# Rotary score products over all 128 rows, and SwiGLU blocks turned by VectorE and ScalarE instead of TensorE

## The chip, the cores and the metric

The kernel runs on one core of a Trainium2 chip. The metric is the device time of one execution in microseconds (us); the times shown are medians of several runs, and one further execution was taken with the hardware profiler. Five engines appear: TensorE (PE in the profile, its weight loads PEld), VectorE (DVE), ScalarE (ACT), GpSimd (POOL) and SyncE (SP), which issues the weight loads from memory. Each engine works through its own list of instructions in the order of that list, and waits where an instruction needs another engine's result or a free buffer.

## What is computed

One layer of an encoder on 256 tokens of width 2048, all in fp32. The layer has two SwiGLU half steps with an inner width of 5632, and between them a mixer (a gated linear recurrence, and an attention with rotary positions) and a cross attention. The two parts that matter here:

```python
def swiglu_half_step(x, pre_g, w_gate, w_up, w_down, post_g):
    h = rms_norm(x, pre_g)
    y = (jax.nn.silu(h @ w_gate) * (h @ w_up)) @ w_down
    return x + FFN_RESIDUAL_WEIGHT * rms_norm(y, post_g)

...
    q_nope, q_pe = q[..., :QK_NOPE], q[..., QK_NOPE:]          # 128 and 64 columns per head, 16 heads
    q_pe = rotary(q_pe, cos[:, :, None, :], sin[:, :, None, :])
    k_pe = rotary(k_pe, cos, sin)                              # one k_pe for all heads
...
        s = jnp.einsum('bqhd,bkhd->bhqk', q_blk, k, preferred_element_type=jnp.float32) * scale
```

A head's score is thus the sum of a product over 128 features and of one over 64 rotary features.

## The kernel before

**Weights.** Every weight tile is 128 x 1024 fp32 (512 KB). `feed` loads it through SP's queue (`raw`, four buffers), ScalarE rounds it to `whi` (L98), VectorE computes the rest `wlo` = raw - whi (L99). `whi` and `wlo` have three buffers each. A product is three matmuls, high by high (L128), low by high (L129) and high by low (L130). One weight tile feeds 12 matmuls of 512 columns in `gemm`; such a dozen is called a group here. Since there are three buffers, ScalarE can round the tile of a group when TensorE has ended the group three before it.

**SwiGLU.** `ffn` goes through 22 blocks of 256 inner columns in two segments, 12 and then 10. A block is one `gemm` named `gu` of 8 groups, with gate columns in the left half of a bank and up columns in the right. ScalarE applies silu (`sg`, L285), VectorE multiplies (`h`, L286), once for each half of the tokens. The next product contracts over the inner columns, so `h` (tokens in rows) has to be turned to `hT` (inner columns in rows). Before the change TensorE does that with four 128 x 128 transposes into a PSUM bank (L290), and `part_split` makes the rounded `fh` (ScalarE, L169) and the rest `fl` (VectorE, L170). After a segment's blocks, four `gemm` named `dn` contract over all its inner columns, 12 groups each in the first segment and 10 in the second; the last block of a segment is needed in the last group of each. There are two half steps, so 44 blocks.

**Rotary scores.** `query_pe` leaves the turned rotary queries of two heads in one 128-row tile, one head in rows 0 to 63 and the other in rows 64 to 127. `key_pe` leaves the turned rotary key twice, in the upper and in the lower 64 rows of `kpeT`. `attend` handles four heads at a time. For each head and each half of the queries (128 or 256 keys) it adds two fp32 products in the same bank: one over 128 rows (L543) and one over the head's 64 rows (L544). A softmax follows on VectorE and ScalarE (L546 to L557), then TensorE transposes the probabilities (L565).

**What sets the order.** A scheduler orders each engine's list when the program is built; `high_priority` lets the weight chain go first, and `issue_after(x)` puts instructions behind instruction x in an engine's list.

Of the kernel before, what the change touches and what calls it, by code (L numbers as in the profile page):

```python
# [9 lines left out]
F32 = mybir.dt.float32  # L10
# [4 lines left out]
AF = mybir.ActivationFunctionType  # L15
# [3 lines left out]
P = 128  # L19
# [18 lines left out]
class Layer:  # L38
    def __init__(self, ctx, tc, A):
        self.tc, self.nc, self.A = tc, tc.nc, A  # L40
        nc = self.nc
        ep = lambda name, bufs, **k: ctx.enter_context(tc.tile_pool(name=name, bufs=bufs, **k))
        self.cst = ep("cst", 1)
        self.small = ep("small", 4)
        self.wraw = ep("wraw", 4)
        self.wsp = ep("wsp", 3)
        self.xp = ep("xp", 4)
        self.hp = ep("hp", 4)
        self.sl = ep("sl", 1)
        self.t2 = ep("t2", 6)  # L50
        self.jk = ep("jk", 1)
        self.gb = ep("gb", 2)
        self.pg = ep("pg", 4, space=bass.MemoryType.PSUM)
        self.pm = ep("pm", 4, space=bass.MemoryType.PSUM)
        self.n = 0
        self.plan, self.at, self.ready = [], 0, 0
        self.spare = {}
        self.last_mm = None
        self.q = []
        self.pending = []  # L60
        self.ident = self.cst.tile([P, P], F32, name="ident")
        make_identity(nc, self.ident)
        self.gc = self.cst.tile([P, NGC], F32, name="gc")
        nc.gpsimd.dma_start(out=self.gc, in_=A["gcol"])
# [20 lines left out]
    def feed(self, ahead):  # L85
        nc = self.nc
        while self.ready < min(self.at + ahead, len(self.plan)):
            src = self.plan[self.ready]
            spare = self.ready in self.spare
            n = src.shape[-1]  # L90
            raw = self.wraw.tile([P, n], F32, name=self.nm("raw"), tag="raw")
            nc.sync.dma_start(out=raw, in_=src)
            if spare:
                hi, lo = self.slot(self.spare[self.ready], "whi", F32R), self.slot(self.spare[self.ready], "wlo", F32R)
            else:
                hi = self.wsp.tile([P, n], F32R, name=self.nm("whi"), tag="whi")
                lo = self.wsp.tile([P, n], F32R, name=self.nm("wlo"), tag="wlo")
            nc.scalar.activation(hi, raw, AF.Copy)  # L98
            nc.vector.tensor_tensor(lo, raw, hi.bitcast(F32), ALU.subtract)  # L99
            self.q.append((hi, lo))  # L100
            self.ready += 1
# [9 lines left out]
    def gemm(self, act, k0, k1, name="g", head=0, tail=0, warm=0):  # L111
        nc = self.nc
        ps = [self.pg.tile([P, 512], F32, name=self.nm(name), tag="g") for _ in range(2)]
        if warm:
            self.keep_warm(ps[1], warm)
        n = (k1 - k0) // 2
        groups = ([range(head)] if head else []) + [range(i, i + 1) for i in range(head, n - tail)] + ([range(n - tail, n)] if tail else [])
        for grp in groups:
            if grp[0] >= head and (grp[0] - head) % 2 == 0:
                self.settle(1)  # L120
            w = [self.weights(self.pending and grp[0] > head) for _ in grp]
            ks = [k0 + 2 * t + c for t in grp for c in range(2)]
            order = [(k, m) for k in ks for m in range(2)] if len(ks) == 2 else [(k, m) for m in range(2) for k in ks]
            for k, m in order:
                wh, wl = w[(k - ks[0]) // 2]
                c = slice(512 * ((k - k0) % 2), 512 * ((k - k0) % 2) + 512)
                ah, al = act(k, m)
                nc.tensor.matmul(ps[m], lhsT=ah, rhs=wh[:, c], start=(k == k0), stop=False)  # L128
                nc.tensor.matmul(ps[m], lhsT=ah, rhs=wl[:, c], start=False, stop=False)  # L129
                self.last_mm = nc.tensor.matmul(ps[m], lhsT=al, rhs=wh[:, c], start=False, stop=(k == k1 - 1))  # L130
        self.settle()
        return ps
# [40 lines left out]
    def gain_split(self, hi, lo, pieces):  # L173
        nc = self.nc
        for o, ps, g in pieces:
            ins = nc.scalar.activation(hi[:, o], ps, AF.Identity, scale=self.gc[:, g : g + 1])
        for o, ps, g in pieces:
            self.last_lo = nc.vector.scalar_tensor_tensor(lo[:, o], ps, self.gc[:, g : g + 1], hi[:, o].bitcast(F32), ALU.mult, ALU.subtract)  # L178
        return ins

    def block_T(self, hi, lo, x, gcols=None, scale=None):
        for half in range(2):
# [83 lines left out]
    def ffn(self, st, which, aside=None):  # L266
        nc = self.nc
        act, r = self.halves(st[0], st[1]), st[2]
        ys = [None] * 4
        ss, ry = self.sm(8, "ssy"), []  # L270
        for si, (b0, b1) in enumerate(SEG):
            quads = []
            for b in range(b0, b1):
                ps = self.gemm(act, 0, KC, "gu", head=SKEW if b == 0 else 0, warm=WARM if b == 0 else 0)
                if (b - b0) % 2 == 0:
                    tag = "A" if len(quads) < 4 else "B"
                    hi, lo = self.slot(tag, "fh", F32R), self.slot(tag, "fl", F32R)
                    quads.append((hi, lo))
                if b == 0 and aside:
                    with self.tc.issue_after(self.last_lo.ins):  # L280
                        aside()
                h = self.tmp("h")
                for m in range(2):
                    sg = self.tmp("sg")
                    nc.scalar.activation(sg[:, :256], ps[m][:, :256], AF.Silu, scale=r[m])  # L285
                    nc.vector.scalar_tensor_tensor(h[:, m * 256 : m * 256 + 256], ps[m][:, 256:], r[m], sg[:, :256], ALU.mult, ALU.mult)  # L286
                pt = self.bank("pT")
                for c in range(2):
                    for m in range(2):
                        nc.tensor.transpose(pt[:, c * 256 + m * P : c * 256 + m * P + P], h[:, m * 256 + c * P : m * 256 + c * P + P], self.ident)  # L290
                s = slice(512 * ((b - b0) % 2), 512 * ((b - b0) % 2) + 512)
                self.part_split(hi[:, s], lo[:, s], pt)
            fa = self.halves([q[0] for q in quads], [q[1] for q in quads])
            for j in range(4):
                ps = self.gemm(fa, 0, 2 * (b1 - b0), "dn", tail=TAIL if si == 1 and j == 3 else 0)
                if si == 0:
                    ys[j] = self.slot("G", "y")
                    for m in range(2):
                        nc.scalar.activation(ys[j][:, m * 512 : m * 512 + 512], ps[m], AF.Copy)
                else:  # L300
                    g = self.load_gain(which, j)
                    for m in range(2):
                        yv = ys[j][:, m * 512 : m * 512 + 512]
                        nc.vector.tensor_tensor(yv, ps[m], yv, ALU.add)
                        ry.append(self.postnorm_block(j, m, g, yv, yv, ss, 0.5))
        return ys, ry[-2:]
# [60 lines left out]
    def mixer_consts(self):  # L367
        nc, v, c = self.nc, self.nc.vector, self.cst
# [20 lines left out]
        m, e0, e1 = (c.tile([P, 16], F32, name=n) for n in ("lbm", "lbe0", "lbe1"))  # L389
# [16 lines left out]
        v.tensor_copy(pf, pi)  # L406
        fr = c.tile([P, 32], F32, name="freq")
        nc.gpsimd.dma_start(out=fr, in_=self.A["invf"].to_broadcast([P, 32]))
        ang, n, tail, w = (c.tile([P, 64], F32, name=s) for s in ("ang", "angn", "angt", "angw"))
        for m_ in range(2):  # L410
            v.tensor_scalar(ang[:, 32 * m_ : 32 * m_ + 32], fr, pf[:, m_ : m_ + 1], None, ALU.mult)
        magic = 12582912.0
# [66 lines left out]
    def key_pe(self, act, r):  # L479
# [21 lines left out]
        pt = self.bank("pT")  # L501
        for m in range(2):
            nc.tensor.transpose(pt[:, m * P : m * P + P], k2[:, m * P : m * P + P], self.ident)
        self.kpeT = self.cst.tile([P, 256], F32, name="kpeT")
        nc.vector.tensor_copy(self.kpeT, pt[:, :256])

    def query_pe(self, ps):
        nc = self.nc
# [22 lines left out]
    def attend(self, g, qn, kn, qpe, value):  # L531
# [2 lines left out]
        probs = []  # L534
        for h in range(4):
            c = 256 * h
            rows = slice(64 * (h % 2), 64 * (h % 2) + 64)
            pc = 256 * ((4 * g + h) // 2 % 4)
            ps = self.bank("sc")
            for m, n0 in ((0, 0), (1, P)):  # L540
                w = P + P * m
                o = ps[:, n0 : n0 + w]
                nc.tensor.matmul(o, lhsT=qn[:, c + m * P : c + m * P + P], rhs=kn[:, c : c + w], start=True, stop=False)  # L543
                nc.tensor.matmul(o, lhsT=qpe[rows, pc + m * P : pc + m * P + P], rhs=self.kpeT[rows, :w], start=False, stop=True)  # L544
            s = self.tmp("s")
            nc.vector.scalar_tensor_tensor(s[:, :384], ps[:, :384], scale, self.amask, ALU.mult, ALU.add)  # L546
            mx, sums = self.sm(2, "mx"), self.sm(2, "su")
# [451 lines left out]
```

## Time and profile before

| | |
|---|---|
| median of 3 runs | 2651.07 us (2650.95 to 2651.12) |
| profiled execution | 2651.14 us, of which the span from first to last instruction is 2649.1 us |
| mean granted clock of TensorE | 0.999 of full speed |
| busy: PE / DVE / ACT / POOL | 2622.8 / 1497.3 / 1311.8 / 13.2 us |
| chain that ended last | PE 96%, DVE 2%, DMA 1%, ACT 1% |
| DMA | 481.39 MB, 182 GB/s on the mean |

The page's busy times are sums over an engine's instructions, where overlapping ones count once. A matmul's duration in a row holds the time from its start to its modelled end, and matmuls overlap; what one costs is read from the distance between starts. A row of the timeline gives the start, the length, engine, line and operation, and in brackets how long the engine was idle before, and what ended that.

### The profile page before, as it was taken

How to read it: one execution, taken by the hardware profiler on the slowest of the kernel's cores; microseconds unless marked ns; L12 is line 12 of the kernel's file. 1: busy time of each engine (PE TensorE's matmuls, PEld its weight loads, DVE VectorE, ACT ScalarE, POOL GpSimd, SP SyncE). 2: the span in 40 equal slices, each digit the busy share in tenths (PEclk: the TensorE clock that was granted, in tenths of full speed). 3: DMA queues.
4: the chain of work that ended last, by engine and by line, in shares of the span. 5: the costliest groups of instructions: out<-in, count | busy, mean ns of one | idle time of the engine just before them, and what ended most of it. 6: DMA issues, size and time to landing. Idle time of an engine off the chain costs nothing.

```text
span 2649.1 us, 33984 instructions
## 1 busy us (share of the span) xinstructions
PE 2622.8 (99%) x13136; PEld 2215.3 (84%) x13136; DVE 1497.3 (57%) x2004; ACT 1311.8 (50%) x1750; POOL 13.2 (0%) x36
## 2 busy tenths in 40 slices
PE   9999999999999999999999999999999999999998
PEld 7888888888888888889989988889788888888886
DVE  6555444554576544447577575657655554455555
ACT  5444444444455444346666664555644444444443
POOL 0000000000000000000000000000000000000000
PEclk9999999999999999999999999999999999999999
DMA  6655555555654346555545545665455556655564
GB/s 230 191 188 187 190 196 192 188 188 189 202 171 144 111 155 195 191 191 160 167 154 165 168 161 189 205 205 178 149 193 191 188 188 193 195 191 188 189 194 161
DMA packets 133714, 481.39 MB, mean 182 GB/s; under 512 B 15024, under 2 KB 15040, under 8 KB 133552
## 3 DMA queue, kind: packets, MB, share of 16 engines
q1 hardware_dynamic: 131472, 473.49, 55.4%
q0 software_dynamic: 1504, 4.68, 0.6%
q8 instruction: 103, 1.69, 0.3%
q10 hardware_dynamic: 576, 1.05, 0.1%
q14 instruction: 59, 0.48, 0.1%
HBM read 477.06 MB, written 2.10 MB: 181 GB/s over the span
## 4 chain that ended last, share of the span: by engine, by line
PE 96%; DVE 2%; DMA 1%; ACT 1%; issue 0%; SPq 0%; DVEq 0%; ACTq 0%
PE gu L130 12%; PE gu L129 12%; PE gu L128 12%; PE dn L128 6%; PE dn L129 6%; PE dn L130 6%; PE gate L130 2%; PE gate L128 2%; PE gate L129 2%; PE wo L129 1%; PE wo L130 1%; PE wo L128 1%; PE hf L352 1%; PE hf L351 1%; PE hf L350 1%; PE hv L129 1%
## 5 line engine op out<-in xcount | busy, mean ns | idle before, releaser
L99 DVE TENSOR_TENSOR wlo<-raw,whi 128x1024 fp32r<-128x1024 f32 x893 | 1092.5, 1225 | 1045.4 <-ACT whi L98 1044.3
L98 ACT ACTIVATE whi<-raw 128x1024 fp32r<-128x1024 f32 x893 | 945.9, 1060 | 1084.0 <-PE gu L130 444.9
L129 PE MATMUL gu<-wlo,hh 128*128 128x512 f32 x1408 | 552.1, 392 | 1.4 <-DVE wlo L99 1.4
L130 PE MATMUL gu<-whi,hl 128*128 128x512 f32 x1408 | 549.1, 390 | 0.7 <-DVE hl L178 0.7
L128 PE MATMUL gu<-whi,hh 128*128 128x512 f32 x1408 | 496.6, 393 | 1.8 <-ACT whi L98 1.5
L128 PEld LDWEIGHTS gu<-whi,hh 128*128 128x128 f32 x1408 | 263.9, 188 | 60.2 <-ACT whi L98 2.1
L130 PEld LDWEIGHTS gu<-whi,hl 128*128 128x128 f32 x1408 | 264.4, 188 | 55.7 <-DVE hl L178 1.5
L129 PEld LDWEIGHTS gu<-wlo,hh 128*128 128x128 f32 x1408 | 264.5, 188 | 55.0 <-DVE wlo L99 2.2
L129 PE MATMUL dn<-wlo,fh 128*128 128x512 f32 x704 | 274.2, 390 | 0.0
L130 PE MATMUL dn<-whi,fl 128*128 128x512 f32 x704 | 274.0, 389 | 0.0
L128 PE MATMUL dn<-whi,fh 128*128 128x512 f32 x704 | 247.1, 390 | 0.0
L128 PEld LDWEIGHTS dn<-whi,fh 128*128 128x128 f32 x704 | 132.1, 188 | 27.8
L130 PEld LDWEIGHTS dn<-whi,fl 128*128 128x128 f32 x704 | 132.2, 188 | 27.3
L129 PEld LDWEIGHTS dn<-wlo,fh 128*128 128x128 f32 x704 | 132.2, 188 | 27.1
L129 PE MATMUL gate<-wlo,hh 128*128 128x512 f32 x256 | 100.7, 394 | 0.0
L130 PE MATMUL gate<-whi,hl 128*128 128x512 f32 x256 | 100.1, 391 | 0.0
L128 PE MATMUL gate<-whi,hh 128*128 128x512 f32 x256 | 91.8, 391 | 0.0
L351 PE MATMUL hf<-hl,whi 128*128 128x256 f32 x256 | 72.5, 284 | 0.0
L351 PE MATMUL hq<-hl,whi 128*128 128x256 f32 x256 | 72.4, 284 | 0.0
L350 PE MATMUL hf<-hh,whi 128*128 128x256 f32 x256 | 72.3, 283 | 0.0
L350 PE MATMUL hq<-hh,whi 128*128 128x256 f32 x256 | 72.1, 283 | 0.0
L352 PE MATMUL hf<-hh,wlo 128*128 128x256 f32 x256 | 71.8, 283 | 0.0
(358 smaller groups left out, 3544.3 us busy)
## 6 DMA issues: line engine op xcount, KB each, us to landing
raw<-in_ffn_gu_dram SPq DMA_DIRECT2D x352, 512.0 KB, 3.4
raw<-in_win_dram SPq DMA_DIRECT2D x208, 512.0 KB, 3.5
raw<-in_ffn_dn_dram SPq DMA_DIRECT2D x176, 512.0 KB, 3.5
raw<-in_wbb_dram SPq DMA_DIRECT2D x32, 512.0 KB, 3.4
raw<-in_wba_dram SPq DMA_DIRECT2D x32, 512.0 KB, 3.5
raw<-in_wo_dram SPq DMA_DIRECT2D x32, 512.0 KB, 3.6
gb<-in_grow_dram POOLq DMA_DIRECT2D x16, 256.0 KB, 4.6
raw<-in_qup_n_dram SPq DMA_DIRECT2D x8, 512.0 KB, 3.4
```

Source lines behind the costliest of these rows:

```text
L98: nc.scalar.activation(hi, raw, AF.Copy)
L99: nc.vector.tensor_tensor(lo, raw, hi.bitcast(F32), ALU.subtract)
L128: nc.tensor.matmul(ps[m], lhsT=ah, rhs=wh[:, c], start=(k == k0), stop=False)
L129: nc.tensor.matmul(ps[m], lhsT=ah, rhs=wl[:, c], start=False, stop=False)
L130: self.last_mm = nc.tensor.matmul(ps[m], lhsT=al, rhs=wh[:, c], start=False, stop=(k == k1 - 1))
L350: nc.tensor.matmul(o, lhsT=wh[:, c], rhs=ah, start=first, stop=False)
L351: nc.tensor.matmul(o, lhsT=wh[:, c], rhs=al, start=False, stop=False)
L352: nc.tensor.matmul(o, lhsT=wl[:, c], rhs=ah, start=False, stop=last)
```

## The change

Two parts.

1. **SwiGLU blocks.** The four TensorE transposes of a block and their PSUM bank go. `turn` does one VectorE transpose of the 128 x 512 tile `h` to `hb`, which turns each 32 x 32 square in place, and 16 ScalarE copies of 32 rows x 128 elements, which put the squares where they belong in `hT`. The copies wait in the list `later`: four of them are issued behind the rounding of group 3's weights of the next `gemm`, four each behind those of groups 4, 5 and 6, and `part_split`, now from SBUF, behind that of group 7.
2. **Rotary scores.** `kpeT` becomes 128 x 512: left half with the key in rows 0 to 63 and zeros below, right half with zeros above and the key in rows 64 to 127. The second product runs over all 128 rows of both heads' queries, and the zeros take the other head out.

To make room, the four small tiles of the angle computation become slices of one temporary tile.

```diff
-            nc.scalar.activation(hi, raw, AF.Copy)
+            self.last_hi = nc.scalar.activation(hi, raw, AF.Copy)
...
             w = [self.weights(self.pending and grp[0] > head) for _ in grp]
+            if self.later and grp[0] >= 3:
+                with self.tc.issue_after(self.last_hi.ins):
+                    self.later.pop(0)()
...
+    def turn(self, h, hi, lo):
+        nc = self.nc
+        b, o = self.tmp("hb"), self.tmp("hT")
+        nc.vector.transpose(b, h)
+        bv = b.rearrange("p (m c q t) -> p m c q t", m=2, c=2, q=4)
+        ov = o.rearrange("p (c m x t) -> p m c x t", c=2, m=2, x=4)
+
+        def strips(x):
+            for q in range(4):
+                nc.scalar.activation(ov[32 * q : 32 * q + 32, :, :, x, :], bv[32 * x : 32 * x + 32, :, :, q, :], AF.Copy)
+
+        self.later += [lambda x=x: strips(x) for x in range(4)] + [lambda: self.part_split(hi, lo, o)]
...
-                pt = self.bank("pT")
-                for c in range(2):
-                    for m in range(2):
-                        nc.tensor.transpose(pt[:, c * 256 + m * P : c * 256 + m * P + P], h[:, m * 256 + c * P : m * 256 + c * P + P], self.ident)
                 s = slice(512 * ((b - b0) % 2), 512 * ((b - b0) % 2) + 512)
-                self.part_split(hi[:, s], lo[:, s], pt)
+                self.turn(h, hi[:, s], lo[:, s])
...
-        ang, n, tail, w = (c.tile([P, 64], F32, name=s) for s in ("ang", "angn", "angt", "angw"))
+        wk = self.tmp("ang")
+        ang, n, tail, w = (wk[:, 64 * i : 64 * i + 64] for i in range(4))
...
-        self.kpeT = self.cst.tile([P, 256], F32, name="kpeT")
-        nc.vector.tensor_copy(self.kpeT, pt[:, :256])
+
+        self.kpeT = self.cst.tile([P, 512], F32, name="kpeT")
+        nc.gpsimd.memset(self.kpeT, 0.0)
+        for h in range(2):
+            nc.vector.tensor_copy(self.kpeT[64 * h : 64 * h + 64, 256 * h : 256 * h + 256], pt[64 * h : 64 * h + 64, :256])
...
-            rows = slice(64 * (h % 2), 64 * (h % 2) + 64)
+            kc = 256 * (h % 2)
...
-                nc.tensor.matmul(o, lhsT=qpe[rows, pc + m * P : pc + m * P + P], rhs=self.kpeT[rows, :w], start=False, stop=True)
+                nc.tensor.matmul(o, lhsT=qpe[:, pc + m * P : pc + m * P + P], rhs=self.kpeT[:, kc : kc + w], start=False, stop=True)
```

TensorE's list is, instruction by instruction, the old one without the 176 transposes L290. SP's list is the same. VectorE's and ScalarE's lists change at the blocks alone, and VectorE's at `kpeT`, where two copies of 64 rows stand for one of 128. POOL gets one memset, ahead of the first gain load that has to wait.

ScalarE, from the silu of a SwiGLU block to that of the next (`whi` roundings of weights, `sg` silu, `fh` rounded inner activations), before:

```order
L285 ACTIVATE sg_807<-gu_658,ry_379 128x256
L98 ACTIVATE whi_860<-raw_858 128x1024
L285 ACTIVATE sg_810<-gu_659,ry_393 128x256
L98 ACTIVATE whi_878<-raw_876 128x1024
L98 ACTIVATE whi_896<-raw_894 128x1024
L169 ACTIVATE fh_804<-pT_813 128x512
L98 ACTIVATE whi_914<-raw_912 128x1024
L98 ACTIVATE whi_932<-raw_930 128x1024
```

The same place now (`hb` is VectorE's output, `hT` the turned tile):

```order
L305 ACTIVATE sg_832<-gu_665,ry_379 128x256
L99 ACTIVATE whi_881<-raw_879 128x1024
L305 ACTIVATE sg_835<-gu_666,ry_393 128x256
L99 ACTIVATE whi_899<-raw_897 128x1024
L197 ACTIVATE hT_839<-hb_838 32x2x2x32 x4
L99 ACTIVATE whi_921<-raw_919 128x1024
L197 ACTIVATE hT_839<-hb_838 32x2x2x32 x4
L99 ACTIVATE whi_943<-raw_941 128x1024
L197 ACTIVATE hT_839<-hb_838 32x2x2x32 x4
L99 ACTIVATE whi_965<-raw_963 128x1024
L197 ACTIVATE hT_839<-hb_838 32x2x2x32 x4
L99 ACTIVATE whi_987<-raw_985 128x1024
```

Behind each of four weight roundings stand four copies now, and the first of these is the only one that depends on a fresh result of VectorE.

VectorE at the same place, now (`wlo` is the rest of a weight tile):

```order
L306 SCALAR_TENSOR_TENSOR h_831<-gu_665,ry_379,sg_832 128x256
L100 TENSOR_TENSOR wlo_882<-raw_879,whi_881 128x1024
L306 SCALAR_TENSOR_TENSOR h_831<-gu_666,ry_393,sg_835 128x256
L191 STREAM_TRANSPOSE hb_838<-h_831 128x512
L100 TENSOR_TENSOR wlo_900<-raw_897,whi_899 128x1024
L100 TENSOR_TENSOR wlo_922<-raw_919,whi_921 128x1024
```

The transpose is new, directly behind the second half of `h` and ahead of the next `wlo`; the rest of these rows stood in the same order before.

## Rows read from the trace of the kernel before

**Rows 1.** The page: TensorE's busy time, and the chain that ended last.

```profile
PE 2622.8 (99%) x13136; PEld 2215.3 (84%) x13136; DVE 1497.3 (57%) x2004; ACT 1311.8 (50%) x1750; POOL 13.2 (0%) x36
...
PE 96%; DVE 2%; DMA 1%; ACT 1%; issue 0%; SPq 0%; DVEq 0%; ACTq 0%
```

**Rows 2.** Timeline, ScalarE: silu of two blocks nine apart, evictions of two dn.

```profile
81.91 0.47 ACT L285 ACTIVATE sg<-gu,ry 128x256 f32<-128x256 f32 x1 [0.98 <-PE gu L130]
...
282.45 0.47 ACT L285 ACTIVATE sg<-gu,ry 128x256 f32<-128x256 f32 x1 [0.98 <-PE gu L130]
...
315.62 0.60 ACT L299 ACTIVATE y<-dn 128x512 f32<-128x512 f32 x1 [0.98 <-PE dn L130]
...
413.54 0.60 ACT L299 ACTIVATE y<-dn 128x512 f32<-128x512 f32 x1 [0.98 <-PE dn L130]
```

**Rows 3.** Groups by shape: busy us, mean ns | idle before, releasers.

```profile
L98 ACT ACTIVATE whi<-raw 128x1024 fp32r<-128x1024 f32 x893 | 945.9, 1060 | 1084.0 <-PE gu L130 444.9 <-PE dn L130 232.5 <-PE gate L130 56.7
L285 ACT ACTIVATE sg<-gu,ry 128x256 f32<-128x256 f32 x88 | 40.8, 465 | 41.2 <-PE gu L130 41.2
L169 ACT ACTIVATE fh<-pT 128x512 fp32r<-128x512 f32 x44 | 26.4, 599 | 39.4 <-PE pT L290 39.4
```

**Rows 4.** Timeline around one block's end, VectorE's and ScalarE's rows.

```profile
107.10 0.48 DVE L286 SCALAR_TENSOR_TENSOR h<-gu,ry,sg 128x256 f32<-128x256 f32 x1
...
108.67 1.23 DVE L99 TENSOR_TENSOR wlo<-raw,whi 128x1024 fp32r<-128x1024 f32 x1 [1.10 <-ACT whi L98]
...
107.58 1.06 ACT L98 ACTIVATE whi<-raw 128x1024 fp32r<-128x1024 f32 x1 [1.29 <-PE gu L130]
```

**Rows 5.** Groups by shape that are nearest to the new instructions.

```profile
L527 DVE COPY cp<-kn 128x512 f32<-128x512 f32 x8 | 5.5, 691 | 1.3 <-PE kn L352 1.2
...
L679 ACT ACTIVATE e<-b 128x256 f32<-128x256 f32 x8 | 2.9, 411 | 8.3 <-PE lv L684 8.3
...
L451 ACT ACTIVATE cos<-angw 128x64 f32<-128x64 f32 x2 | 0.4, 248 | 0.0
```

**Rows 6.** Timeline, TensorE: scores of the third four heads, first and last rows.

```profile
894.98 0.38 PE L543 MATMUL sc<-cp,cp 128*128 128x128 f32 x2
895.29 0.48 PE L544 MATMUL sc<-kpeT,qpeT 64*128 64x128 f32 x2
895.71 0.70 PE L543 MATMUL sc<-cp,cp 128*128 128x256 f32 x2
896.34 0.70 PE L544 MATMUL sc<-kpeT,qpeT 64*128 64x256 f32 x2
896.96 0.49 PE L543 MATMUL sc<-cp,cp 128*128 128x128 f32 x2
...
903.23 0.50 PE L128 MATMUL vv<-whi,ch 128*128 128x512 f32 x1
```

**Rows 7.** Timeline, TensorE: fp32 products over 128 rows only, two in one bank.

```profile
881.77 0.60 PE L573 MATMUL po<-pT,cp 128*128 128x256 f32 x2
882.20 0.38 PE L574 MATMUL po<-pT,cp 128*128 128x128 f32 x2
882.42 0.60 PE L573 MATMUL po<-pT,cp 128*128 128x256 f32 x2
```

**Rows 8.** Timeline, TensorE: scores of the first four heads.

```profile
843.53 0.48 PE L544 MATMUL sc<-kpeT,qpeT 64*128 64x128 f32 x2
...
844.57 0.70 PE L544 MATMUL sc<-kpeT,qpeT 64*128 64x256 f32 x4
...
849.17 0.70 PE L544 MATMUL sc<-kpeT,qpeT 64*128 64x256 f32 x2
```

**Rows 9.** Timeline, TensorE: scores of the second four heads, first and last row.

```profile
861.83 0.39 PE L543 MATMUL sc<-cp,cp 128*128 128x128 f32 x2
...
871.96 0.70 PE L544 MATMUL sc<-kpeT,qpeT 64*128 64x256 f32 x2
```

**Rows 10.** Timeline, third four heads: first head's probabilities ready, their transposes.

```profile
902.37 0.54 DVE L557 TENSOR_SCALAR s<-s,su 128x128 f32<-128x128 f32 x2
...
906.18 0.49 PE L565 MATMUL pT<-ident,s 128*128 128x128 f32 x3
```

More of the change, by code (lines that the diff above doesn't have):

```diff
@@ L60, in __init__ @@
         self.pending = []
+        self.later = []
         self.ident = self.cst.tile([P, P], F32, name="ident")
```

## The prediction

> **What bounds the kernel now.** I read the page first: TensorE is busy 2622.8 us of a span of 2649.1, and 96% of the chain that ended last is its own work [rows 1]. So an instruction taken off TensorE's list shortens the run by what it costs there, as long as the engines that take over its work don't make TensorE wait; and an instruction added to VectorE or ScalarE is free as long as it fits into their idle time at that place. The next view is the timeline, for the price of a block in the stage that the change touches. A SwiGLU block lasts from one silu to the silu of the next: nine blocks take 282.45 - 81.91 = 200.54 us, 22.28 each [rows 2]. A dn gemm of the first segment has 12 groups of the same 12 matmuls and no transposes: three of them take 413.54 - 315.62 = 97.92 us, so a group takes 2.72 [rows 2]. Eight groups without transposes would be 21.76 us.
>
> **SwiGLU, what goes.** The difference, 22.28 - 21.76 = 0.52 us, is what the four transposes cost TensorE, with all that they disturb. It holds for a segment's last block too, whose transposes fall into the first dn gemm: that gemm's first eviction comes at 315.62, 33.17 us after the block's silu at 282.45 and so 0.53 more than 32.64 [rows 2]. 44 blocks x 0.52 = **23.0 us off**.
>
> **SwiGLU, what comes.** VectorE gets one transpose of 128 x 512 per block. The trace has no such operation. The nearest row is a copy of the same shape, 0.69 us [rows 5]; I take 0.69. The bounds are 0.48, the 128 x 256 multiplication ahead of it, and 1.23, the weight rest of twice the size [rows 4]. It stands behind the second h, which ends at 107.10 + 0.48 = 107.58, and so ends at 108.3; the next weight rest starts at 108.67 [rows 4] and isn't held up. At 1.23 us it would be, by 0.15 us; that rest ends at 109.9, and its group comes only two groups after the one that began when the rounding was released, at about 107.4 + 2 x 2.72 = 112.8. So about 2.9 us cover it. Without that cover the 44 transposes would cost 30 us.
>
> ScalarE gets 16 copies of 32 rows x 128 elements per block. The nearest rows are 128 x 64 in 0.25 us and a strided 128 x 256 in 0.41 [rows 5]; by elements 128 lie in between, and I take 0.33. Four behind a rounding make 1.06 + 4 x 0.33 = 2.38 us [rows 3], less than the 2.72 of a group, in which ScalarE before waited for TensorE ahead of each rounding (1.29 us in front of the one at 107.58 [rows 4]). At the upper bound the sum is 2.70 and still fits. Per block ScalarE has 8 x 1.06 + 2 x 0.465 + 0.60 = 10.0 us of old work [rows 3], with 5.3 new 15.3 of 21.76. The only new wait is that of the first four copies for the transpose; behind them stands the next rounding. They come up when the rounding of 107.58 ends, at 108.64, after the transpose's 108.3, so they find it done. At 1.23 us it would end at 108.8 and hold them for 0.2 us, which goes under in the idle time ahead of the next rounding. The last block of a segment is turned within the first five slots of its dn gemm behind group 7's rounding, and its result is needed in group 11 or 9, at least two groups (5.4 us) later. All this I cost at nothing. `part_split` only changes its source. The weight loads keep their order and number on SP's queue, and they only come 2% closer in these stages. The memset on POOL lies ahead of every wait for a gain buffer, and the angle tile's operations keep their order: nothing, too.
>
> **Scores, what goes.** Where score products over 128 and over 64 rows alternate, the starts are 0.42 us apart for 128 columns (895.29 to 895.71) and 0.63 for 256 (895.71, 896.34, 896.96) [rows 6]. Two fp32 products over 128 rows that follow each other into one bank take 0.43 for 256 columns and 0.22 for 128 [rows 7]. So each change between the row counts costs about 0.2 us. Four heads without changes would take 4 x 2 x (0.43 + 0.22) = 5.2 us; the third four take 903.23 - 894.98 = 8.25 [rows 6], 3.0 more, for 16 changes. The fourth four have the same rows. In the second four, from 861.83 to 871.96 [rows 9], TensorE does other products in between, but each of the eight 64-row products again stands alone: 16 changes, 3.0 us. In the first four two 64-row products lie side by side twice, and there both take one step (the row of four instructions in 0.63 us [rows 8]): 849.17 + 0.63 - 843.53 = 6.27 us for products that would take 4.57 without changes, 1.7 more [rows 8]. After the change all products have 128 rows and the same number of columns: 1.7 + 3 x 3.0 = **10.7 us off**.
>
> The Trainium skill, "TensorEngine Tiling (Array Packing)", Key Properties, says that a change of the tiling mode drains the engine, with which these pauses agree. The same section speaks against this change: different row tiles work in parallel, so 64-row products of two heads could share the array. The trace shows that in rows 8, and by that rule each pair given up costs one product; here only two pairs were ever neighbours. Had one gone by the drain alone, 4 x 3.0 = 12.0 us would go and the sum would be 2616.1.
>
> What comes: one more copy of a half `kpeT` on VectorE, 3 us before its first use; nothing.
>
> **The sum.** The profiled execution took 2651.14 us, 2.0 of it outside its span, and stands at the median of the runs (2651.07). 2651.1 - 23.0 - 10.7 = **2617.4 us**. A measurement can tell 0.2% here, 5.3 us.
>
> **The rivals.**
> *The softmax takes the place of the pauses.* TensorE would reach the transposes of the probabilities earlier, and these depend on VectorE and ScalarE, which get no faster. For it: a head's products come every 1.3 us instead of 2.1, and the softmax's instructions stay as they are. Against it: the first head's probabilities are ready at 902.37 + 0.54 = 902.91, its transposes start at 906.18 [rows 10], so 3.3 us of cover meet 3.0 us of saving. If the cover were gone in every four heads, 2617.4 to 2628.1, with half of it kept about 2623. Chance 0.11.
> *The pause doesn't come from the row count* but from adding into a bank that was just written. Against it: rows 7 add into one bank with no pause. Then only the blocks count: 2628.1. Chance 0.03.
> *ScalarE becomes the bound (slower).* Four copies may not lie behind a rounding as cheaply as I take it, since only 32 of 128 rows work in each. If a copy takes s, a block needs 10.0 + 16 s. Beyond s = 0.41 the roundings start late within four groups but catch up in the other four; beyond (21.76 - 10.0)/16 = 0.73 TensorE waits for ScalarE in every block. The old time comes back at 0.52 + 10.7/44 = 0.76 us per block, s = 0.78; at 0.80 a block takes 22.8 us, 44 x 1.04 = 46 us more than forecast, 2663. Against it: no ScalarE row of 256 columns or fewer is near that [rows 5]. Chance 0.03; for a stage in between, with late weights at block ends (2630 to 2645), another 0.03.
> The Trainium skill, "VectorE: DVE Perf Modes", Rules for kernel authors, advises TensorE for turning 128 x 128 where PSUM may be the destination, and has VectorE turn 32 x 32 squares alone; the 16 copies are the price of that rule, and this rival is the case in which it holds.
>
> **How the numbers follow.** The forecast keeps 0.80. Its own spread is some 4 us each way: the price per transpose within 0.02 us a block is 1 us, the changes between row counts 2, entries and exits of the score products another 1. Reaching down to 2613 and up to 2626 takes in the likelier part of the first rival; left out are its end and the others, about 0.12. Faster by over 0.2% holds the forecast, the first two rivals and most of the stage in between: 0.96; within 0.2% 0.01; slower 0.03.
>
> **What would show it.** Right: no L290-like row on TensorE; blocks 21.76 us apart in silu starts; copies of 0.25 to 0.41 us that end before the next rounding's release; roundings that still wait for TensorE, not TensorE for them; score starts 0.22 and 0.43 apart; the third four heads in 5.2 us; softmax rows earlier by as much. Wrong: idle time on TensorE put down to whi or wlo in SwiGLU blocks, or to probabilities; a block period above 21.9; a transpose over 4 us.

## The result, and the profile after

The changed kernel takes **2616.86 us** (median of four runs, 2616.6 to 2617.22) against 2651.1 us before: a ratio of 0.9871, 95% interval 0.9853 to 0.9888. The forecast was 2617.4 us. The profiled execution took 2616.6 us with a span of 2614.6, which is 34.5 us less than the span of 2649.1 before; the granted clock is 0.999 again.

The page, TensorE's busy time and the chain that ended last, answers to [rows 1]:

```profile
PE 2588.6 (99%) x12960; PEld 2201.4 (84%) x12960; DVE 1523.7 (58%) x2049; ACT 1519.9 (58%) x2454; POOL 13.6 (1%) x37
...
issue 71%; PE 27%; DVE 1%; DMA 0%; POOL 0%; ACT 0%; DVEq 0%; POOLq 0%; ACTq 0%
```

TensorE lost 176 instructions and 34.2 us of busy time, and still works for 99% of the span. ScalarE gained 208 us of work and VectorE 26, and the span did not notice. The chain's shares are put down differently from before, "issue" in place of PE (time in which nothing that the profile shows was waited for); with TensorE 99% busy I read that as the same bound, and rest nothing on it.

Next the groups by shape (busy us, mean ns of one, idle before it), the weight rounding and the new instructions; the first and the last answer to [rows 3]:

```profile
L99 ACT ACTIVATE whi<-raw 128x1024 fp32r<-128x1024 f32 x893 | 945.7, 1060 | 881.0 <-PE gu L134 223.4 <-PE dn L134 210.5 <-PE gate L134 56.9
...
L197 ACT ACTIVATE hT<-hb 32x128 f32<-32x128 f32 x704 | 216.1, 307 | 9.7 <-DVE hb L191 0.2
...
L191 DVE STREAM_TRANSPOSE hb<-h 128x512 f32<-128x512 f32 x44 | 31.3, 711 | 1.5
...
L173 ACT ACTIVATE fh<-hT 128x512 fp32r<-128x512 f32 x44 | 27.0, 613 | 0.0
```

A copy takes 0.307 us and a transpose 0.711. The roundings' idle time fell from 1084.0 to 881.0 us: that is where the copies went. The copies waited 0.2 us in all for the transposes.

The timeline of ScalarE shows how this looks in one block; silu starts nine blocks apart (the first and the last row) answer to [rows 2], the rest to [rows 4]:

```profile
80.98 0.47 ACT L305 ACTIVATE sg<-gu,ry 128x256 f32<-128x256 f32 x1 [0.98 <-PE gu L134]
...
149.66 1.06 ACT L99 ACTIVATE whi<-raw 128x1024 fp32r<-128x1024 f32 x1 [1.30 <-PE gu L134]
150.62 1.25 ACT L197 ACTIVATE hT<-hb 32x128 f32<-32x128 f32 x4
152.43 1.06 ACT L99 ACTIVATE whi<-raw 128x1024 fp32r<-128x1024 f32 x1 [0.55 <-ACT hT L197]
153.51 1.27 ACT L197 ACTIVATE hT<-hb 32x128 f32<-32x128 f32 x4
155.15 1.06 ACT L99 ACTIVATE whi<-raw 128x1024 fp32r<-128x1024 f32 x1 [0.36 <-ACT hT L197]
156.23 1.26 ACT L197 ACTIVATE hT<-hb 32x128 f32<-32x128 f32 x4
157.82 1.06 ACT L99 ACTIVATE whi<-raw 128x1024 fp32r<-128x1024 f32 x1 [0.33 <-PE gu L134]
...
276.82 0.47 ACT L305 ACTIVATE sg<-gu,ry 128x256 f32<-128x256 f32 x1 [0.98 <-PE gu L134]
```

Nine blocks take 276.82 - 80.98 = 195.84 us, **21.76 each**: eight groups of 2.72 and nothing more. Rounding plus four copies take 149.66 to 151.87, 2.2 us, and some 0.4 us of idle time stays ahead of each next rounding. Two of these waits are put down to the copies (`<-ACT hT L197`), and I first took them for a delay behind copies of about 0.6 us. They aren't: the four roundings start 2.77, 2.72 and 2.67 us apart, at TensorE's pace, and the experiments with more copies have the next rounding start 0.02 us behind the last copy. A wait for several semaphores was put down to the wrong one.

TensorE's timeline of the third four heads, scores and what follows, answers to [rows 6]:

```profile
878.61 0.38 PE L563 MATMUL sc<-cp,cp 128*128 128x128 f32 x2
878.83 0.39 PE L564 MATMUL sc<-kpeT,qpeT 128*128 128x128 f32 x2
879.05 0.60 PE L563 MATMUL sc<-cp,cp 128*128 128x256 f32 x2
879.49 0.59 PE L564 MATMUL sc<-kpeT,qpeT 128*128 128x256 f32 x2
...
883.42 0.60 PE L564 MATMUL sc<-kpeT,qpeT 128*128 128x256 f32 x2
883.66 0.58 PE L132 MATMUL vv<-whi,ch 128*128 128x512 f32 x1
884.08 0.40 PE L133 MATMUL vv<-wlo,ch 128*128 128x512 f32 x1
...
886.70 0.49 PE L585 MATMUL pT<-ident,s 128*128 128x128 f32 x3
```

Starts are 0.22 and 0.43 apart, without a pause. From the first score to the second `vv` product are 884.08 - 878.61 = 5.47 us; before they were 903.56 - 894.98 = 8.58, by [rows 6] and this row of the same timeline of the kernel before:

```profile
903.56 0.40 PE L129 MATMUL vv<-wlo,ch 128*128 128x512 f32 x1
```

VectorE's row that ends the first head's softmax, now, answers to [rows 10]:

```profile
883.86 0.54 DVE L577 TENSOR_SCALAR s<-s,su 128x128 f32<-128x128 f32 x2
```

The first head's probabilities are ready at 883.86 + 0.54 = 884.40, and their transposes start at 886.70: 2.3 us of the 3.3 us of cover are left, and TensorE doesn't wait.

**Where the 34.5 us come from**, by starts on TensorE: 11.4 us are gone by the first product behind the first half step (748.69, now 737.30); 11.2 between the first score (838.69, now 827.32) and the first `gate` product (933.27, now 910.66); 0.3 from there to the second half step (a wait for a weight rest in the cross attention, 0.57 us before and 0.35 now, is most of it; why it is shorter is open); and 11.55 in that half step (last `dn` product 2638.02, now 2603.55).

### The profile page after: what moved, and what is told of

It is laid out like the page before. It is cut to its first block, busy times and chain, and to the rows that moved or that the text cites. A ratio compares the mean times of both kernels' runs of the same rounds, so it can differ in the third digit from the quotient of the medians.

```text
span 2614.6 us, 34383 instructions
## 1 busy us (share of the span) xinstructions
PE 2588.6 (99%) x12960; PEld 2201.4 (84%) x12960; DVE 1523.7 (58%) x2049; ACT 1519.9 (58%) x2454; POOL 13.6 (1%) x37
## 4 chain that ended last, share of the span: by engine, by line
issue 71%; PE 27%; DVE 1%; DMA 0%; POOL 0%; ACT 0%; DVEq 0%; POOLq 0%; ACTq 0%
PE gu L134 6%; PE gu L133 6%; PE gu L132 6%; PE dn L132 3%; PE dn L134 3%; PE dn L133 3%; DMA gb<-in_grow_dram 0%; DVE y L350 0%; POOL gb L275 0%; DVE wlo L100 0%; DVE rt L153 0%; PE pT L206 0%; DVE yo L280 0%; DVE ry L157 0%; DVE hl L182 0%
## 5 line engine op out<-in xcount | busy, mean ns | idle before, releaser
L99 ACT ACTIVATE whi<-raw 128x1024 fp32r<-128x1024 f32 x893 | 945.7, 1060 | 881.0 <-PE gu L134 223.4
L197 ACT ACTIVATE hT<-hb 32x128 f32<-32x128 f32 x704 | 216.1, 307 | 9.7 <-DVE hb L191 0.2
```

Of the source, the lines that this page charges most:

```text
L99: self.last_hi = nc.scalar.activation(hi, raw, AF.Copy)
L197: nc.scalar.activation(ov[32 * q : 32 * q + 32, :, :, x, :], bv[32 * x : 32 * x + 32, :, :, q, :], AF.Copy)
```

## The experiments

Each time is a median of four to eleven runs, and its ratio is to the kernel before on the same chip (medians 2650.5 to 2650.9 us).

### The two parts apart

The first takes the score part back:

```diff
-                nc.tensor.matmul(o, lhsT=qpe[:, pc + m * P : pc + m * P + P], rhs=self.kpeT[:, kc : kc + w], start=False, stop=True)
+                nc.tensor.matmul(o, lhsT=qpe[rows, pc + m * P : pc + m * P + P], rhs=self.kpeT[rows, :w], start=False, stop=True)
```

> Only the SwiGLU part of the change; the scores as before, 64-row products and all. Theory (the two parts add up, 23.0 us for the blocks): 2628.1 us, silu starts 21.76 apart, third four heads 8.25 us as in the kernel before. Rival (part of the gain of the blocks is the loss of something that the scores give back, or the pause in the scores is not of the row count): a time off by more than 1 us from 2628.1, or third four heads other than 8.2 to 8.3 us.

Measured: **2628.38 us** (ratio 0.9915, 0.9901 to 0.9928). TensorE's timeline of the third four heads, first row and the row behind the last:

```profile
883.96 0.38 PE L560 MATMUL sc<-cp,cp 128*128 128x128 f32 x2
...
892.21 0.50 PE L132 MATMUL vv<-whi,ch 128*128 128x512 f32 x1
```

8.25 us, as before. The second keeps only the score part (the same lines, in the kernel before):

> Only the score part of the change; the SwiGLU blocks turned by TensorE as before. Theory (each change between 64 and 128 rows costs about 0.2 us, and the softmax does not take it back): 2651.1 - 10.7 to 11.2 = 2639.9 to 2640.4 us, third four heads 5.2 us. Rival (softmax becomes the bound, here as there): 2643 us or more, with TensorE waiting for the probabilities.

Measured: **2639.32 us** (ratio 0.9956, 0.9944 to 0.9969). Alone the parts give 22.5 and 11.6 us, 34.0 together; the whole change gives 34.2. Neither takes from the other by more than the runs can tell. The pause is of the row count: the second run still adds two products into one bank, and only the rows of one have changed.

### Scores over 64 rows, side by side

Is it the change of row count that costs, or the 64 rows? Here two heads' 128-row products come first, then their 64-row products, neighbours in different row halves (one head in rows 0 to 63, the other in rows 64 to 127) and banks. The fours do the same with four heads.

```diff
+                for part in range(2):
+                    for m, n0 in ((0, 0), (1, P)):
...
+                        for i in range(2):
...
+                            if part == 0:
+                                nc.tensor.matmul(o, lhsT=qn[:, c + m * P : c + m * P + P], rhs=kn[:, c : c + w], start=(m == 0), stop=False)
+                            else:
+                                nc.tensor.matmul(o, lhsT=qpe[rows, pc + m * P : pc + m * P + P], rhs=self.kpeT[rows, :w], start=False, stop=(m == 1))
```

> The changed SwiGLU part, but scores over 64 rows again, in another order: two heads' four products over 128 rows first, then both heads' 64-row products, the two heads side by side in different row halves and different banks. Theory A (row halves work in parallel, and a change between row counts costs 0.2 us): a pair of heads takes 1.31 + 0.65 + 2 x 0.2 = 2.36 us in place of 2.62 in the changed kernel, 8 pairs: about 2 us less than the changed kernel, 2614.8 us. Theory B (they do not work in parallel): 2.62 + 0.4 per pair, 3 us more than the changed kernel, 2620 us. Both: TensorE does not wait for probabilities; the first head's scores come one head later (1 us), of a cover of 2.3 us.

> As the pairs, with all four heads of a group: eight 128-row products, then eight 64-row products, neighbours in different row halves. Theory A (parallel): four heads take 2.62 + 1.31 + 0.4 = 4.3 us in place of 5.24, 4 x 0.9 = 3.7 us less than the changed kernel, 2613.2 us, provided the softmax keeps up. Theory B (not parallel): 5.24 + 0.4, 2618.5 us. Softmax rival: the first head's scores come about 2 us later than in the changed kernel and its probabilities with them, against a cover of 2.3 us; if that is gone, TensorE waits and up to 4 x 1 to 2 us come back: 2615 to 2620 us, with TensorE's wait at the first transposes of probabilities put down to VectorE or ScalarE.

Measured: pairs **2616.60 us** (0.9871, 0.9857 to 0.9884), fours **2618.18** (0.9877, 0.9862 to 0.9892). By the total both theories A are wrong; the timeline says otherwise of their mechanism. TensorE in the pairs, a part of the second four heads and then the third four (a row can hold both widths):

```profile
856.57 0.92 PE L568 MATMUL sc<-kpeT,qpeT 64*128 64x128 f32 x4
857.42 0.92 PE L566 MATMUL sc<-cp,cp 128*128 128x128 f32 x4
...
879.84 1.47 PE L566 MATMUL sc<-cp,cp 128*128 128x128 f32 x8
881.24 0.93 PE L568 MATMUL sc<-kpeT,qpeT 64*128 64x128 f32 x8
882.09 1.58 PE L566 MATMUL sc<-cp,cp 128*128 128x128 f32 x8
883.60 0.93 PE L568 MATMUL sc<-kpeT,qpeT 64*128 64x128 f32 x8
884.46 0.50 PE L133 MATMUL vv<-wlo,ch 128*128 128x512 f32 x1
```

In the third four, eight instructions of 64 rows take 0.85 us, the 0.2 of the change in it; in the second four, four of them take the same 0.85. So two row halves do work in parallel, and the third four heads take 4.62 us. The Trainium skill, "TensorEngine Tiling (Array Packing)", Key Properties, has it that different tiles run in parallel, and that a change of the mode drains: these rows agree with both. The gain is lost in the second four: there the list has one head's products after the other's, with changes between (why the scheduler put them so wasn't tested). Over all sixteen heads the distances from each score instruction to TensorE's next sum to 19.7 us in the changed kernel, 19.8 in the pairs and 20.8 in the fours. In the pairs the second four heads take 6.17 us of it where the changed kernel takes 4.67, which is what the other three gain together (1.5 us); in the fours the second and the fourth four lose. TensorE waits for no probabilities in either, so the softmax rival isn't the cause.

If that is right, holding the 64-row products behind the last 128-row product of their pair, or four, brings the gain:

```diff
-                                nc.tensor.matmul(o, lhsT=qn[:, c + m * P : c + m * P + P], rhs=kn[:, c : c + w], start=(m == 0), stop=False)
+                                last = nc.tensor.matmul(o, lhsT=qn[:, c + m * P : c + m * P + P], rhs=kn[:, c : c + w], start=(m == 0), stop=False)
...
+                                with self.tc.issue_after(last.ins):
```

> The pairs again (64-row products, two heads side by side in different row halves), with the 64-row products held behind the last 128-row product of their pair in TensorE's list, since in the pairs the scheduler had put the heads of the second four heads one by one. In the pairs the third four heads took 4.62 us against 5.24 of the changed kernel, and the second four lost what was gained there. Theory (row halves work in parallel; only the order spoiled the gain): about 0.6 us for each four heads, 2.0 to 2.5 us less than the changed kernel, 2614.5 us. Rival (waiting for the second head costs as much as is gained, in transposes and values that are put between other products, with a change of product kind each): 2616 to 2617 us as before.

> The fours again, all eight 64-row products of four heads held behind the last 128-row product. In the fours the third four heads took 4.22 us against 5.24, and the second and fourth four were put head by head. Theory: 4 x 0.9 to 1.0 = 3.7 us less than the changed kernel, 2613.2 us. Rival (128-row products that lie apart between projections cost 0.1 us on each return, and probabilities come later, among the gate products): 2615 to 2618 us.

Measured: **2615.24 us** for the pairs (0.9867, 0.9851 to 0.9884) and **2614.07** for the fours (0.9862, 0.9848 to 0.9877). Against the changed kernel's profile the spans are 1.5 and 3.1 us shorter. TensorE in the held fours, the end of the second four heads' scores:

```profile
858.11 0.82 PE L566 MATMUL sc<-cp,cp 128*128 128x128 f32 x4
858.86 1.58 PE L569 MATMUL sc<-kpeT,qpeT 64*128 64x128 f32 x16
860.37 0.39 PE L366 MATMUL qn<-ch,whi 128*128 128x256 f32 x1
```

Eight products (two instructions each) in 1.51 us, where the changed kernel's over 128 rows take 4 x 0.65 = 2.6. The distances sum to 17.5 us in the held pairs and 15.4 in the held fours; of the 4.3 us that the fours gain there, 1.2 go elsewhere (the 128-row products now lie apart among projections, which may be why). So the held order beats the changed kernel in the trace, by less than the 5.3 us that the prediction lets a measurement tell; set against the medians of before beside them, 2650.5 and 2651.1 us, the fours' gain is 2.2 us. One comparison is closer: the kernel with seven copies, below, has the changed kernel's TensorE list, lost no time, and ran on the same chip as the two held orders. Its runs took 2616.57 to 2617.31 us, the held pairs' 2614.86 to 2615.94 and the held fours' 2613.59 to 2614.66; the ranges don't overlap.

### How much ScalarE and VectorE can take

All 16 copies behind the rounding of group 3:

```diff
-        self.later += [lambda x=x: strips(x) for x in range(4)] + [lambda: self.part_split(hi, lo, o)]
+        def whole():
+            for x in range(4):
+                strips(x)
+
+        self.later += [whole, lambda: self.part_split(hi, lo, o)]
```

> The changed kernel with all 16 copies of a block behind the rounding of group 3, in place of four behind each of four roundings. Theory (late roundings cost nothing as long as they make it up within the three weight buffers): 16 x 0.31 = 5 us in one piece make the next rounding late by about 5 + 1.06 + 0.6 - 2.72 = 3.9 us, against a cover of about 2.9 us (two groups of 2.72 less the rounding and the weight rest), so TensorE waits up to 1 us in a block: 0 to 44 us over the changed kernel, most likely about 18 (2635 us). Rival (only the sum of ScalarE's work per block counts, since it fits into 21.76 us): no change, 2617 us within 1.

Measured: **2625.99 us** (0.9908, 0.9894 to 0.9922): 9 us over the changed kernel, half of what was thought likeliest. That only the sum per block counts is out. ScalarE's timeline:

```profile
152.02 1.06 ACT L99 ACTIVATE whi<-raw 128x1024 fp32r<-128x1024 f32 x1 [1.30 <-PE gu L134]
152.99 5.08 ACT L197 ACTIVATE hT<-hb 32x128 f32<-32x128 f32 x16
158.09 1.06 ACT L99 ACTIVATE whi<-raw 128x1024 fp32r<-128x1024 f32 x1
```

The next rounding was due at 152.02 + 2.72 = 154.74 and starts 3.35 us late. A block takes 21.93 us (silu from 82.83 to 280.22 in nine blocks), 0.17 more than 21.76: about 3.2 us of lateness are covered, and TensorE waits for the rest. The three buffers make that plausible: two groups less one rounding and one weight rest are 5.44 - 1.06 - 1.23 = 3.15 us.

Then each copy twice (eight behind a rounding), three of four twice (seven), and each three times (twelve):

```diff
-            for q in range(4):
+            for q in [q for q in range(4) for _ in range(2)]:
```

> The changed kernel with each of the 16 copies of a block done twice, the second time over the first with the same values; eight behind each rounding. It stands for a copy of 0.61 us in the prediction's law. Theory (TensorE waits only where ScalarE's work per block passes 21.76 us): 10.0 + 32 x 0.31 = 20 us of 21.76, no change, 2617 us within 2, roundings late within the four groups (1.06 + 8 x 0.31 = 3.5 us, and some 0.6 us of waiting behind the copies, against 2.72). Rival (the lateness of four groups, 4 x 0.8 to 1.4 us, goes past the cover of about 2.9 us before it can be made up): TensorE waits 0.3 to 2.7 us a block, 2630 to 2735 us.

> The changed kernel with each copy done three times, the repeats over the first with the same values; twelve behind each rounding. It stands for a copy of 0.92 us, past the point of 0.73 from which the prediction's rival has ScalarE as the bound. Theory: 10.0 + 48 x 0.31 = 24.9 us per block, 3.1 over 21.76, 44 x 3.1 = 138 us over the changed kernel, 2755 us, and TensorE waiting for the rounded weights; with 0.6 us of waiting behind each four groups' copies 2860. If ScalarE were not the bound (rival): 2617 us.

> The changed kernel with three of each four strip copies done twice (the repeat over the first with the same values), so that seven lie behind each rounding: between the changed kernel's four and the eight of the copies done twice, which took the time up by 35 us. Theory from these runs (TensorE waits for what the last of four late roundings is late beyond a cover of 3.15 us): each group costs 1.06 + 7 x 0.329 + 0.03 = 3.39 us against 2.72, the fifth rounding is late by 4 x 0.67 = 2.7 us, under the cover: no change, 2617 us within 1. Rival (each copy more costs in proportion, 35 us for 16 a block): three quarters of 35, 2643 us.

Measured: twice **2651.61 us** (1.0004, 0.9995 to 1.0013), seven **2616.91** (0.9873, 0.9858 to 0.9888), three times **2838.1** (1.0708, 1.0694 to 1.0723). ScalarE's timeline with each copy twice, the first group and the last rounding of the row, and the wait that TensorE has there, about once in a block (from the list of waits: us in total, times, longest):

```profile
154.40 1.06 ACT L99 ACTIVATE whi<-raw 128x1024 fp32r<-128x1024 f32 x1 [1.30 <-PE gu L134]
155.37 2.62 ACT L197 ACTIVATE hT<-hb 32x128 f32<-32x128 f32 x8
158.01 1.06 ACT L99 ACTIVATE whi<-raw 128x1024 fp32r<-128x1024 f32 x1
...
169.24 1.06 ACT L99 ACTIVATE whi<-raw 128x1024 fp32r<-128x1024 f32 x1
```

```profile
PE gu L133 <- DVE wlo L100: 20.4, 43, 0.9
```

Five roundings from 154.40 to 169.24 take 14.84 us where four groups take 10.88: the fifth is 3.96 us late, and a block takes 22.53 us (silu from 105.94 to 151.00 in two blocks), 0.77 more than 21.76. Again 3.2 us are covered. With seven copies the same rows:

```profile
149.66 1.06 ACT L99 ACTIVATE whi<-raw 128x1024 fp32r<-128x1024 f32 x1 [1.30 <-PE gu L134]
150.62 2.29 ACT L197 ACTIVATE hT<-hb 32x128 f32<-32x128 f32 x7
...
163.18 1.06 ACT L99 ACTIVATE whi<-raw 128x1024 fp32r<-128x1024 f32 x1
```

13.52 us, 2.64 late, under the cover: no change. The expectation of the copies done twice was wrong, that of the seven, made from the first two, right. So there is a step: 12 more copies a block are free, and 16 more cost 35 us.

With each copy three times ScalarE is the bound, and its row shows a wait that wasn't expected:

```profile
121.11 0.46 ACT L305 ACTIVATE sg<-gu,ry 128x256 f32<-128x256 f32 x1
121.46 1.06 ACT L99 ACTIVATE whi<-raw 128x1024 fp32r<-128x1024 f32 x1
123.86 3.64 ACT L197 ACTIVATE hT<-hb 32x128 f32<-32x128 f32 x11 [1.34 <-DVE hb L191]
...
148.00 0.46 ACT L305 ACTIVATE sg<-gu,ry 128x256 f32<-128x256 f32 x1
```

A block takes 148.00 - 121.11 = 26.89 us: 15.8 of copies, 9.7 of older work, and 1.34 in which ScalarE waits for a transpose that its own late silu, and a weight rest that stands between on VectorE, released late. Expected were 24.9 us per block; the wait is most of what was missed, and copies 0.33 us apart in place of 0.31 are 0.9 more.

Last, VectorE's transpose four times:

```diff
-        nc.vector.transpose(b, h)
+        for _ in range(4):
+            nc.vector.transpose(b, h)
```

> The changed kernel with VectorE's transpose of each block done four times, the repeats over the first with the same values: 2.84 us in place of 0.71, just under the cover of 2.9 us that the prediction gives it. Theory (covered): no change, 2617 us, at most 2 us more; the first four copies wait for it, and the weight rest behind it is late by up to 2 us without TensorE noticing. Rival (the transpose is on the path, because the weight rest behind it is needed earlier than thought): up to 44 x 2.1 = 94 us more, 2711 us.

Measured: **2616.8 us** (0.9873, 0.9860 to 0.9887). VectorE's timeline:

```profile
106.50 1.46 DVE L192 STREAM_TRANSPOSE hb<-h 128x512 f32<-128x512 f32 x2
107.89 1.18 DVE L100 TENSOR_TENSOR wlo<-raw,whi 128x1024 fp32r<-128x1024 f32 x1
108.99 1.45 DVE L192 STREAM_TRANSPOSE hb<-h 128x512 f32<-128x512 f32 x2
110.36 1.18 DVE L100 TENSOR_TENSOR wlo<-raw,whi 128x1024 fp32r<-128x1024 f32 x1
```

No change, but not the test that was meant: the scheduler put a weight rest in the middle, so none had all 2.84 us ahead of it, and it moved the first copies one group on. It shows that 94 us of transposes more find room on VectorE; that 2.9 us in one piece would be covered wasn't tried.

## Why the prediction was right

- **What bounds the kernel** held: 34.2 us less of TensorE's busy time, 34.5 us less span.
- **SwiGLU, 23.0 us off**: 11.4 + 11.55 = 22.9 by starts, and a period of 21.76 as worked out. The part alone gave 22.5.
- **VectorE's transpose at 0.69, covered**: 0.711, and the copies waited 0.2 us for it in 44 blocks.
- **ScalarE's copy at 0.33, four behind a rounding in 2.38 of 2.72 us**: 0.307; 2.2 us, and idle time is left in every group.
- **Scores, 10.7 us off**: mis-sized by 0.5, since 11.2 went. The term was read up to the start of the product behind the scores, and so held the last change, back to 128 rows, only in part: up to the second `vv` product 8.58 - 5.47 = 3.1 us go in the third four heads, where 3.0 stood, and as much in the second and the fourth. In the first four 1.9 us go, where 1.7 stood: from their first score to the `qn` product behind them are 850.02 - 838.69 = 11.33 us before and 836.75 - 827.32 = 9.43 now. With the 0.3 us between the half steps that makes the 0.8 us by which the span fell more than 33.7.
- **The softmax rival**: of 3.3 us of cover 2.3 are left, where 3.3 against 3.0 had been set. That the softmax gets no faster was wrong. VectorE's timeline of the kernel before, in the third four heads, shows why (the first head's negation, L550, stands behind the second head's first step, L546, and so on):

```profile
899.16 0.56 DVE L546 SCALAR_TENSOR_TENSOR s<-sc,amask 128x384 f32<-128x384 f32 x1 [0.89 <-PE sc L544]
899.63 0.16 DVE L550 TENSOR_SCALAR mx<-mx 128x2 f32<-128x2 f32 x1
...
901.25 0.56 DVE L546 SCALAR_TENSOR_TENSOR s<-sc,amask 128x384 f32<-128x384 f32 x1 [0.88 <-PE sc L544]
```

  The first head's softmax waited twice for the scores of the heads behind it. These come 1.31 us apart now and not 2.09, so its probabilities are ready 5.8 us after the first score (884.40 - 878.61), not 7.9 (902.91 - 894.98): 2.1 us of the 3.1 are given back.
- **The same-bank rival** fell: products into one bank run at 0.22 and 0.43 without a pause.
- **ScalarE as the bound**: here a step of the prediction failed, though the result didn't hang on it. It let late roundings catch up freely until a copy of s = 0.73 us, the point where the sum of a block no longer fits. The runs put in its place the lateness that piles up over four groups: about 3.2 us are covered (two runs, 3.35 - 0.17 and 3.96 - 0.77). With 0.03 us from the last copy to the next rounding, TensorE begins to wait where 4 x (1.06 + 4 s + 0.03 - 2.72) = 3.2, at s = 0.61. The old time came back at s = 2.63 / 4 = 0.66, not 0.78. With s = 0.31 the change is far from either. By the same sum with 3.2 + 0.52, the SwiGLU part alone would lose its gain from s = 0.64 on, an estimate. The rule of the Trainium skill that the prediction names there, TensorE for turning 128 x 128 where PSUM may be the destination ("VectorE: DVE Perf Modes", Rules for kernel authors), would pay in this kernel only beyond that point.

## What to carry to other kernels

Price a stage by its period: here the distance between the same instruction of two blocks, less the matmuls alone, gave the gain to 0.1 us in 23. Work moved to an idle engine was free here up to a step that the buffers set; it isn't the sum per block that decides but how late the last of several late instructions is, so spread the work, and count its lateness against the buffers' cover. On TensorE, keep products of one row count together; a padding with zeros does that simply, and row halves side by side did it better here by 1.5 to 3 us, with the order of the list held.

## What the runs showed that was not expected

- Half-height products of two heads side by side take half the time: 16 instructions of 64 rows in 1.51 us, a change of row count in it, against 4 in 0.85 with one where a head stands alone.
- The copy of 32 rows x 128 elements takes 0.307 us, and four behind each other only 1.26: their starts are 0.32 apart, next to no gap.
- A releaser named in the trace can be wrong by one semaphore: 39.5 us of waits, 87 times, stand against copies on ScalarE that had ended, while in the block shown the starts lie on TensorE's 2.72 us grid.
